# The weight split's subtractions all on VectorE, GpSimd without them: a two-block transformer on one core

## The chip, the cores and the metric

The kernel runs on 1 core of one Trainium2 chip. The metric is the device time of a launch in microseconds (us), median of the runs. A core has TensorE (PE in the rows; PEld is its weight load), VectorE (DVE), ScalarE (ACT), GpSimd (POOL), SyncE (SP, which issues the DMAs here) and 16 DMA engines.

## The reference, cut to what matters

Two blocks of two layers follow each other on 256 tokens of 1024 channels, all in float32. The second block holds the places that the prediction speaks of:

```python
for l in range(DEPTH):
    mod = cond @ ada_w[l] + ada_b[l]
    sh1, sc1, g1, sh2, sc2, g2, sh3, sc3, g3 = jnp.split(mod, N_MOD, axis=-1)
    hn = _modulate(_rms_norm(h, norm_g[l, 0]), sh1, sc1)
    h = h + 0.5 * g1[:, None, :] * _swiglu(hn, ffn1_w_in[l], ffn1_w_out[l])
    hn = _modulate(_rms_norm(h, norm_g[l, 1]), sh2, sc2)
    z = hn @ w_in[l]
    ...
    mixed = jnp.concatenate([o_a, o_b, o_c, o_d], axis=-1)
    h = h + g2[:, None, :] * (mixed @ w_out[l])
    hn = _modulate(_rms_norm(h, norm_g[l, 2]), sh3, sc3)
    h = h + 0.5 * g3[:, None, :] * _swiglu(hn, ffn2_w_in[l], ffn2_w_out[l])
```

`o_a` is a differential attention (two softmaxes, one subtracted from the other), `o_b` a causal depthwise convolution of 31 taps with a layer norm, `o_c` a spatial gating within chunks of 128 tokens, `o_d` an attention with forget gates. The first block (three attentions side by side, a gated sum and a squared-ReLU MLP) is computed ahead of it in the same way.

## The kernel before, in words

**Weights.** Activations lie feature-major, 128 channels by 256 tokens to a tile. Every weight is read from HBM once, in the order of use. `_plan` and `_subs` cut the weights into 627 parts of at most 1024 columns. A part goes through three steps. `load_to` (line 214) issues its DMA from SyncE into a tile `raw`, of which there are 5. `split_to` (line 223) makes two tiles of it, of 4 buffers each: `wh` is a rounded copy, a cast on ScalarE (line 231), and `wl` is the rest, `raw - wh` (line 233). `mm3` (line 284) then multiplies three times into the same PSUM bank: `wh` by the high part of the activation, `wh` by its low part, and `wl` by the high part. So TensorE needs `wl` of a part in the third matmul of its first group.

**Which engine subtracts.** Line 233 stands on GpSimd where `(i + 1) % prog["pool"] == 0`, else on VectorE. `prog["pool"]` is set along the program: no part on GpSimd in the first stretch, then every third, and in a feed-forward part (`ffn`, line 1108, at the last of its four output products) every part after the first feed-forward of a layer and every second after the second one. So throughout a mixer all parts are subtracted on GpSimd, until line 1378, near its end, sets every third again.

**What runs ahead.** `chunk` (line 268) hands out the parts of a product and has each part split 3 parts ahead of its use. After each part `fill` gives a step to the background pieces that are due. A framework puts the instructions of each engine into one order, by when it reckons that each can start, and it sets the semaphores. An engine works through its own order without overtaking. Where a part's subtraction stands thus moves its neighbours too.

**The mixer** (`mixer`, line 1124) runs between the two feed-forwards of a layer, twice in all. It reads two small tensors (`v2` at line 1127, `ws` at 1128), clears the convolution's input (`yv`, line 1130, held behind the last subtraction that went to VectorE), and takes from `v2` the products `lp` (line 1137). `normalised` (line 1019) writes the normalised input `xn` (line 1037). TensorE then makes the projections, and beside them run as background pieces: `qknorm` (line 1162; the tiles `qu`, `qr`, `qk`), the convolution `conv` (line 1174; 62 steps on `cv` on VectorE, then the matmuls `cc`), `diff` (line 1223; scores `ds`, probabilities `dp`, factors `drc`), `fox` (line 1266; decays `lfr`, scores `fs`) and `spatial` (line 1329). The last projection is `mv`, in 48 matmuls of 512 columns. Before the mixer `gated_update` (line 1057) adds the feed-forward's product `fd` into `x`, and TensorE sums squares into `nrm` for the norm.

**ada.** During the feed-forwards `ada_step` (line 535) takes a 512 KB tile by a DMA of SyncE and multiplies it on VectorE, 144 times in all. Line 172 is the matmul that all products go through, line 185 is `scalar_tensor_tensor`, line 188 a multiplication, line 191 an addition, line 194 a subtraction and line 600 a maximum, all on VectorE.

Of the kernel before, what the change touches and what calls it, by code (L numbers as in the profile page):

```python
# [15 lines left out]
ALU = mybir.AluOpType  # L16
# [10 lines left out]
POOL_EVERY = 3  # L27
# [51 lines left out]
def _subs():  # L79
    """The parts in which the weights are loaded and split: (chunk, first k tile, k tiles, columns, offset)."""  # L80
    subs, o = [], 0
    for j, (_, _, _, kk, _, cc) in enumerate(_plan()):
        per = max(1, SUB_COLS // cc)
        for k in range(0, kk, per):
            n = min(per, kk - k)
            subs.append((j, k, n, cc, o))
            o += P * n * cc
    return subs
# [34 lines left out]
def tile_model(ctx: ExitStack, tc: tile.TileContext, xT: bass.AP, pos: bass.AP, cvec: bass.AP, wst: bass.AP,  # L123
# [55 lines left out]
    def base_table(last):  # L179
        """Back to the table with both Exp and Ln once the given activation is issued."""  # L180
        with tc.issue_after(last.ins):
            nc.scalar.preload_act_table_set("natural_log_exp_and_others")
# [29 lines left out]
    prog = {"raw": 0, "split": 0, "chunk": 0, "fill": 0, "turn": 0, "pool": POOL_EVERY, "ada": 0}  # L212
# [10 lines left out]
    def split_to(s, ahead=5):  # L223
        while prog["split"] < min(s, len(subs)):
# [7 lines left out]
            eng = nc.gpsimd if (i + 1) % prog["pool"] == 0 else nc.vector  # L232
            ins = eng.tensor_tensor(out=wl[:, :n * cc], in0=src, in1=wh[:, :n * cc].bitcast(F32), op=ALU.subtract)  # L233
            if eng is nc.vector:
                prog["dve"] = ins.ins
# [5 lines left out]
    def fill():  # L241
        """One step of each background part that is due."""
        prog["fill"] += 1
        for g in list(bgs):
            if prog["fill"] >= due[g]:
                step(g)

    def step(g):
        """A part yields the number of fills until its next step."""
        try:  # L250
            due[g] = prog["fill"] + next(g)
        except StopIteration:
            bgs.remove(g)
# [37 lines left out]
    def gemm(chunks, ah, al, outs, klast, koff=0, after=None):  # L291
        """Feature-major product; outs[m] = (bank, half) for column tile m of each chunk."""
# [9 lines left out]
    def gemm_last(c, a, banks, klast, done):  # L302
        """The last part of a product, bank by bank, each followed by what takes it up."""
# [9 lines left out]
    def gemm_tok(chunks, ah, al, outs, klast):  # L313
        """Token-major product; outs[t] = (bank, first column)."""
# [7 lines left out]
    def gemm_shift(c, xa, banks, after):  # L322
        """The product with an unnormalised activation; the shift's products follow in two more columns."""
# [40 lines left out]
    def accumulate(n, j, t):  # L364
        """Sums of squares over the channels of a partition; the last part stays apart."""
# [15 lines left out]
    class Act:  # L381
        """A feature-major activation of n tiles as high and low float32r parts."""
# [13 lines left out]
    class Shifted:  # L396
        """An activation scaled per channel, in two parts, with two more columns for the shift."""
# [32 lines left out]
    prog["pool"] = len(subs)  # L430
# [8 lines left out]
    prog["pool"] = POOL_EVERY  # L439
# [151 lines left out]
    def pv(bank, v, pts):  # L591
        """Two heads; columns of each part: keys0 x (q0, q1), keys1 x q1."""
# [11 lines left out]
    def causal_scores(parts):  # L604
        """Masked scores of several heads: (bank, queries, keys) of each."""
# [14 lines left out]
    # =================== block 1 ===================  # L620
# [3 lines left out]
    for l in range(L):  # L624
# [361 lines left out]
        for half in range(2):  # L986
# [5 lines left out]
            for m in range(4):  # L992
# [5 lines left out]
                elif half:  # L998
                    if m == 2:
                        prog["pool"] = 3  # L1000
# [13 lines left out]
    # =================== block 2 ===================  # L1014
# [4 lines left out]
    def normalised(dst, l, i, first=False):  # L1019
        """rmsnorm(x) * g * (1 + scale) + shift in two parts, and the factor of the unnormalised product."""  # L1020
# [52 lines left out]
    def ffn(l, f, i, xa, first=False):  # L1073
# [5 lines left out]
        prog["pool"] = POOL_EVERY  # L1079
# [24 lines left out]
        for m in range(4):  # L1104
            if m == 2:
                prog["ada"] = 0
            if m == 3:
                prog["pool"] = 1 if i == 0 else 2
# [15 lines left out]
    def mixer(l, xa):  # L1124
# [253 lines left out]
        prog["pool"] = 3  # L1378
# [156 lines left out]
```

## Time and profile before

| | us |
|---|---|
| median of 3 runs | 2057.26 |
| lowest and highest of them | 2048.43, 2058.85 |
| profiled execution, span of its instructions | 2054.9 |

The profiled execution has no time of its own beside its span. The median lies 2.4 us above the span. In a row of the profile, "x" and a number is a count, a "<-" in an instruction leads from its output to its inputs, and a "<-" behind an idle time names the instruction that ended it. PEclk is the share of TensorE's full clock that was granted: 1.00 is 2.4 GHz and 0.50 is 1.2 GHz. A count of a window is of the instructions that touch it.

### The profile page before, as it was taken

How to read it: one execution, taken by the hardware profiler on the slowest of the kernel's cores; microseconds unless marked ns; L12 is line 12 of the kernel's file. 1: busy time of each engine (PE TensorE's matmuls, PEld its weight loads, DVE VectorE, ACT ScalarE, POOL GpSimd, SP SyncE). 2: the span in 40 equal slices, each digit the busy share in tenths (PEclk: the TensorE clock that was granted, in tenths of full speed). 3: DMA queues.
4: the chain of work that ended last, by engine and by line, in shares of the span. 5: the costliest groups of instructions: out<-in, count | busy, mean ns of one | idle time of the engine just before them, and what ended most of it. 6: DMA issues, size and time to landing. Idle time of an engine off the chain costs nothing. (4 is left out here: it accounts for less than half of the span.)

```text
span 2054.9 us, 38413 instructions
## 1 busy us (share of the span) xinstructions
PE 1966.4 (96%) x15570; PEld 1894.0 (92%) x15570; DVE 1480.6 (72%) x2076; ACT 1045.8 (51%) x1584; POOL 717.9 (35%) x339
## 2 busy tenths in 40 slices
PE   8999999999999999999999978998999998789999
PEld 7989999999989999999999966898999998679999
DVE  6778778696667778699877598888574446968443
ACT  5656555445556545345444446644454444455442
POOL 3232242323331343334223653422332246443222
PEclk9999999999999999999999989999999999899999
DMA  7545556885445656886667522388546554324553
GB/s 248 169 165 207 209 175 244 306 317 206 144 144 190 227 188 227 309 295 216 242 260 252 183 93 93 124 289 302 183 151 215 179 178 134 108 93 165 184 175 125
DMA packets 114946, 406.52 MB, mean 198 GB/s; under 512 B 12880, under 2 KB 14672, under 8 KB 114768
## 3 DMA queue, kind: packets, MB, share of 16 engines
q1 hardware_dynamic: 114768, 404.06, 56.6%
q8 instruction: 122, 2.00, 0.4%
q14 instruction: 56, 0.46, 0.1%
HBM read 402.96 MB, written 1.05 MB: 197 GB/s over the span
## 5 line engine op out<-in xcount | busy, mean ns | idle before, releaser
L233 POOL TENSOR_TENSOR wl<-raw,wh 128x1024 fp32r<-128x1024 f32 (+2 forms) x253 | 635.0, 2514 | 1257.7 <-ACT wh L231 1182.8
L231 ACT CAST wh<-raw 128x1024 fp32r<-128x1024 f32 (+1 forms) x627 | 641.4, 1030 | 614.7 <-PE fd L172 113.4
L233 DVE TENSOR_TENSOR wl<-raw,wh 128x1024 fp32r<-128x1024 f32 (+1 forms) x374 | 497.3, 1335 | 248.6 <-ACT wh L231 246.1
L172 PE MATMUL f<-hh,wl 128*128 128x256 f32 x1280 | 363.9, 285 | 4.9 <-POOL wl L233 4.0
L172 PE MATMUL f<-hl,wh 128*128 128x256 f32 x1280 | 364.2, 285 | 3.2 <-DVE hl L194 2.9
L172 PE MATMUL f<-hh,wh 128*128 128x256 f32 x1280 | 363.1, 284 | 4.3 <-ACT hh L203 3.1
L185 DVE SCALAR_TENSOR_TENSOR ada<-ada,cond 128x1024 f32<-128x1024 f32 x144 | 227.8, 1585 | 94.9 <-DMA ada<-ada_dram 94.6
L172 PEld LDWEIGHTS f<-hh,wl 128*128 128x128 f32 x1280 | 246.8, 193 | 6.4 <-POOL wl L233 4.6
L172 PEld LDWEIGHTS f<-hl,wh 128*128 128x128 f32 x1280 | 246.9, 193 | 4.8 <-DVE hl L194 4.8
L172 PEld LDWEIGHTS f<-hh,wh 128*128 128x128 f32 x1280 | 246.6, 193 | 5.1 <-ACT hh L203 3.7
L172 PE MATMUL fd<-hidh,wl 128*128 128x256 f32 x704 | 200.4, 285 | 4.0 <-DVE wl L233 3.5
L172 PE MATMUL fd<-hidh,wh 128*128 128x256 f32 x704 | 200.0, 284 | 0.6 <-DVE x L185 0.6
L172 PE MATMUL fd<-hidl,wh 128*128 128x256 f32 x704 | 199.9, 284 | 0.0
L172 PE MATMUL pr<-hh,wh 128*128 128x256 f32 x672 | 194.8, 290 | 0.0
L172 PE MATMUL pr<-hh,wl 128*128 128x256 f32 x672 | 190.1, 283 | 0.0
L172 PE MATMUL pr<-hl,wh 128*128 128x256 f32 x672 | 190.0, 283 | 0.0
L172 PE MATMUL dn<-hidh,wl 128*128 128x256 f32 x512 | 146.2, 285 | 3.6 <-DVE wl L233 3.6
L172 PE MATMUL u<-hh,wl 128*128 128x256 f32 x512 | 145.9, 285 | 2.6 <-DVE wl L233 2.6
L172 PE MATMUL u<-hh,wh 128*128 128x256 f32 x512 | 145.9, 285 | 0.0
L172 PE MATMUL dn<-hidh,wh 128*128 128x256 f32 x512 | 145.6, 284 | 0.0
L172 PE MATMUL dn<-hidl,wh 128*128 128x256 f32 x512 | 145.5, 284 | 0.0
L172 PE MATMUL u<-hl,wh 128*128 128x256 f32 x512 | 145.5, 284 | 0.0
(474 smaller groups left out, 4786.1 us busy)
## 6 DMA issues: line engine op xcount, KB each, us to landing
raw<-wst_dram SPq DMA_DIRECT2D x599, 512.0 KB, 4.0
ada<-ada_dram SPq DMA_DIRECT2D x144, 512.0 KB, 5.0
raw<-wst_dram SPq DMA_DIRECT2D x22, 256.0 KB, 2.8
raw<-wst_dram SPq DMA_DIRECT2D x4, 390.0 KB, 3.0
R<-ret_dram SPq DMA_DIRECT2D x2, 512.0 KB, 7.7
out_dram<-x SPq DMA_DIRECT2D x8, 128.0 KB, 3.3
C<-cst_dram SPq DMA_DIRECT2D x1, 896.0 KB, 7.7
v<-vec_dram SPq DMA_DIRECT2D x2, 448.0 KB, 5.7
```

The source lines that it names most:

```text
L172: nc.tensor.matmul(out, lhsT=lhsT, rhs=rhs, start=grp not in self.open, stop=stop, skip_group_check=True)
L185: nc.vector.scalar_tensor_tensor(out=out, in0=in0, scalar=s, in1=in1, op0=op0, op1=op1, **kw)
L231: nc.scalar.copy(wh[:, :n * cc], src)
L233: ins = eng.tensor_tensor(out=wl[:, :n * cc], in0=src, in1=wh[:, :n * cc].bitcast(F32), op=ALU.subtract)
```

## The change

`POOL_EVERY` and `prog["pool"]` go, with all places that set it. Line 233 becomes a `tensor_tensor` of VectorE for every part, and `prog["dve"]` is the last such subtraction always. Docstrings and comments go too; by that, and by the lines that went, lines stand 1 to 12 lower in number (the subtraction on line 231, `scalar_tensor_tensor` on 184, the matmul on 171).

```diff
@@ -24,7 +24,6 @@
 SUB_COLS = 1024
-POOL_EVERY = 3
 MLA_SCALE = (64 + 32) ** -0.5
...
@@ -203,13 +202,13 @@
...
-    prog = {"raw": 0, "split": 0, "chunk": 0, "fill": 0, "turn": 0, "pool": POOL_EVERY, "ada": 0}
+    prog = {"raw": 0, "split": 0, "chunk": 0, "fill": 0, "turn": 0, "ada": 0}
...
@@ -229,24 +228,22 @@
             wl = wp.tile([P, SUB_COLS], F32R, tag="wl", bufs=4, name=nm("wl"))
             src = raws.pop(i)[:, :n * cc]
             nc.scalar.copy(wh[:, :n * cc], src)
-            eng = nc.gpsimd if (i + 1) % prog["pool"] == 0 else nc.vector
-            ins = eng.tensor_tensor(out=wl[:, :n * cc], in0=src, in1=wh[:, :n * cc].bitcast(F32), op=ALU.subtract)
-            if eng is nc.vector:
-                prog["dve"] = ins.ins
+            ins = tt(out=wl[:, :n * cc], in0=src, in1=wh[:, :n * cc].bitcast(F32), op=ALU.subtract)
+            prog["dve"] = ins.ins
...
@@ -427,7 +424,6 @@
     h = Act(8, "h")
-    prog["pool"] = len(subs)
...
-    prog["pool"] = POOL_EVERY
...
@@ -996,8 +991,6 @@
                 elif half:
-                    if m == 2:
-                        prog["pool"] = 3
...
@@ -1076,7 +1069,6 @@
         gemm_shift(("F" + f, l, 0, 8, 0, 512), xa, b4, lambda: next(nrm))
-        prog["pool"] = POOL_EVERY
...
@@ -1104,8 +1096,6 @@
-            if m == 3:
-                prog["pool"] = 1 if i == 0 else 2
...
@@ -1375,7 +1365,6 @@
-        prog["pool"] = 3
```

In the whole program VectorE's order grows from 1746 to 2022 rows and GpSimd's falls from 316 to 63, with no `wl` left on it. What stays on GpSimd are sums of squares, masks, copies and maxima. ScalarE has 48 table loads where it had 42, three more in each mixer. On SyncE the loads of `raw` that waited for GpSimd to be done with a buffer wait for VectorE, and at 5 places a load of `raw` and a load of `ada` next to it change places.

**VectorE, middle of the mixer of layer 0,** at the normalisation of the second of the four query and key products (`cv` a step of the convolution, `qu` and `qr` the inverse root, `qk` its result). Before:

```order
L185 SCALAR_TENSOR_TENSOR cv_13772<-yv_13554,cw,cv_13772 128x256 x8
L185 SCALAR_TENSOR_TENSOR qu_13970<-qn_13967,eps,qr_13969 128x512
L185 SCALAR_TENSOR_TENSOR cv_13772<-yv_13554,cw,cv_13772 128x256
L185 SCALAR_TENSOR_TENSOR qu_13970<-qu_13970,qr_13969 128x512
L185 SCALAR_TENSOR_TENSOR cv_13772<-yv_13554,cw,cv_13772 128x256
L185 SCALAR_TENSOR_TENSOR qr_13969<-qu_13970,qr_13969 128x512
L185 SCALAR_TENSOR_TENSOR cv_13772<-yv_13554,cw,cv_13772 128x256
L185 SCALAR_TENSOR_TENSOR qk_13741<-qk_13851,V,qr_13969 128x512
```

Now:

```order
L184 SCALAR_TENSOR_TENSOR cv_13772<-yv_13554,cw,cv_13772 128x256 x2
L231 TENSOR_TENSOR wl_13936<-raw_13781,wh_13935 128x1024
L184 SCALAR_TENSOR_TENSOR cv_13772<-yv_13554,cw,cv_13772 128x256 x4
L184 SCALAR_TENSOR_TENSOR qu_13970<-qn_13967,eps,qr_13969 128x512
L231 TENSOR_TENSOR wl_13980<-raw_13815,wh_13979 128x1024
L184 SCALAR_TENSOR_TENSOR qu_13970<-qu_13970,qr_13969 128x512
L184 SCALAR_TENSOR_TENSOR cv_13772<-yv_13554,cw,cv_13772 128x256
L184 SCALAR_TENSOR_TENSOR qr_13969<-qu_13970,qr_13969 128x512
L184 SCALAR_TENSOR_TENSOR cv_13772<-yv_13554,cw,cv_13772 128x256
L184 SCALAR_TENSOR_TENSOR qk_13741<-qk_13851,V,qr_13969 128x512
```

Of the mixer's subtractions 16 (13 of 1024 columns, 2 of 780, 1 of 520) now stand on VectorE between the norm's inverse root and the last step on `cv`; two are seen here. By the same ordering 16 small steps of other pieces (6 on `lfr`, 1 reciprocal, 4 batch-norm statistics, 1 on `drc`, 4 on `dp`) stand ahead of the last step on `cv` where they stood behind it.

**VectorE, from the end of the first feed-forward into the mixer of layer 0** (`x` the update by the product `fd`, `xl` the low part of the scaled input, `lp` the products that read `v2`). Before:

```order
L185 SCALAR_TENSOR_TENSOR x<-fd_13196,hg_164,x 128x256 x2
L185 SCALAR_TENSOR_TENSOR xl_12813<-x,scl_162,xh_12810 128x256 x2
L1130 MEMSET yv_13554 128x576
L188 TENSOR_TENSOR lp_13562<-v_2050_13552 128x32 x2
L1138 TENSOR_REDUCE ls_13563<-lp_13562 128x1 x2
L185 SCALAR_TENSOR_TENSOR x<-fd_13375,hg_164,x 128x256 x2
L188 TENSOR_TENSOR ws_13553<-ws_13553,C 128x128 x3
L185 SCALAR_TENSOR_TENSOR xl_12813<-x,scl_162,xh_12811 128x256
```

Now:

```order
L231 TENSOR_TENSOR wl_13499<-raw_13376,wh_13498 128x1024
L231 TENSOR_TENSOR wl_13529<-raw_13406,wh_13528 128x1024
L1120 MEMSET yv_13554 128x576
L231 TENSOR_TENSOR wl_13590<-raw_13436,wh_13589 128x1024
L184 SCALAR_TENSOR_TENSOR x<-fd_13375,hg_164,x 128x256 x2
L187 TENSOR_TENSOR ws_13553<-ws_13553,C 128x128
L184 SCALAR_TENSOR_TENSOR xl_12813<-x,scl_162,xh_12811 128x256
L187 TENSOR_TENSOR ws_13553<-ws_13553,C 128x128 x3
L184 SCALAR_TENSOR_TENSOR xl_12813<-x,scl_162,xh_12811 128x256
L187 TENSOR_TENSOR lp_13562<-v_2050_13552 128x32 x2
```

The last two updates of `x` stood behind `lp`; now `lp` stands behind them.

**TensorE, end of the projections of the same mixer** (`hh_13579` holds the first four tiles of the input, `hh_13580` the last four; `cc` is the convolution's centring, `tr` a transpose). Before:

```order
L172 MATMUL mv_14402<-wh_14320,hh_13579 128x512
L172 MATMUL mv_14402<-wh_14320,hl_13581 128x512
L172 MATMUL mv_14402<-wl_14321,hh_13579 128x512
L172 MATMUL cc_14453<-cv_13772,C 128x256 x4
L588 MATMUL tr_14461<-C,dp_14092 128x128 x3
L588 MATMUL tr_14466<-C,dp_14092 128x128 x3
L172 MATMUL fs_14471<-fqk_13742 128x128
```

Now:

```order
L171 MATMUL mv_14402<-wh_14435,hh_13580 128x512
L171 MATMUL mv_14402<-wh_14435,hl_13582 128x512
L171 MATMUL mv_14402<-wl_14436,hh_13580 128x512
L171 MATMUL cc_14453<-cv_13772,C 128x256 x4
L583 MATMUL tr_14461<-C,dp_14092 128x128 x3
L583 MATMUL tr_14466<-C,dp_14092 128x128 x3
L171 MATMUL fs_14471<-fqk_13742 128x128
```

Before, `cc` stood after the first 24 of the 48 matmuls of `mv`; now it stands after all 48. The mixer of layer 1 has the same moves at all three places.

## Rows read from the trace of the kernel before

**Rows 1.** The page, part 1: busy us, share of the span, instructions of each engine.

```profile
PE 1966.4 (96%) x15570; PEld 1894.0 (92%) x15570; DVE 1480.6 (72%) x2076; ACT 1045.8 (51%) x1584; POOL 717.9 (35%) x339
```

**Rows 2.** Windows: busy (count) of PE, PEld, DVE, ACT, POOL; PEclk, DMA share, GB/s.

```profile
1600.00:1700.00 100.00, 100.00 (x836) 100.00 (x835) 46.41 (x55) 47.42 (x67) 38.36 (x20) 1.00 0.52 174
1165.00:1305.00 140.00, 114.86 (x772) 101.04 (x772) 121.94 (x237) 73.06 (x148) 68.00 (x27) 0.89 0.30 99
```

**Rows 3.** Waits of TensorE, whole span: us in total, times, longest us.

```profile
PE ds L172 <- DVE qk L185: 17.7, 2, 8.9
PE cc L172 <- DVE cv L185: 9.3, 2, 4.7
PE nrm L172 <- ACT sq L378: 8.0, 5, 2.9
PE fs L172 <- DVE lfr L1273: 6.3, 2, 3.5
...
PE f L172 <- POOL wl L233: 4.0, 2, 2.0
...
PE dn L172 <- DVE wl L233: 3.6, 3, 2.0
PE fd L172 <- DVE wl L233: 3.5, 3, 2.2
```

**Rows 4.** Groups by form, whole span: busy us, mean ns | idle before it, releasers.

```profile
L233 POOL TENSOR_TENSOR wl<-raw,wh 128x1024 fp32r<-128x1024 f32 x236 | 609.5, 2585 | 1227.2 <-ACT wh L231 1152.3 <-DVE hidl L194 29.3 <-DVE Q L188 9.8
L233 DVE TENSOR_TENSOR wl<-raw,wh 128x1024 fp32r<-128x1024 f32 x363 | 489.8, 1354 | 241.6 <-ACT wh L231 239.2 <-PE fd L172 0.3
```

**Rows 5.** Windows, first mixer, 1170.6 to 1252.1: all engines; then line L233 alone (DVE, POOL).

```profile
1170.60:1252.10 81.50, 64.91 (x436) 57.82 (x436) 80.75 (x143) 39.06 (x73) 43.20 (x16) 0.88 0.29 98
...
1170.60:1252.10 81.50, 0.00 (x0) 43.20 (x16) 0.88 0.29 98
```

**Rows 6.** Groups by form of VectorE in 1170.6 to 1252.1.

```profile
L185 DVE SCALAR_TENSOR_TENSOR cv<-yv,cw,cv 128x256 f32<-128x256 f32 x60 | 36.9, 660 | 0.0
L1037 DVE TENSOR_SCALAR xn<-xn,scl,mods 128x256 f32<-128x256 f32 x8 | 9.2, 1200 | 0.0
L185 DVE SCALAR_TENSOR_TENSOR qr<-qu,qr 128x512 f32<-128x512 f32 x4 | 6.9, 1725 | 0.0
L185 DVE SCALAR_TENSOR_TENSOR qu<-qu,qr 128x512 f32<-128x512 f32 x4 | 4.9, 1232 | 0.0
...
L1237 DVE TENSOR_SCALAR drc<-drc,lam 128x2 f32<-128x2 f32 x3 | 2.9, 963 | 0.0
```

**Rows 7.** Timeline of VectorE, single places: start us, us, instruction.

```profile
1219.21 0.68 DVE L185 SCALAR_TENSOR_TENSOR qr<-qu,qr 128x512 f32<-128x512 f32 x1
...
1220.87 2.84 DVE L185 SCALAR_TENSOR_TENSOR cv<-yv,cw,cv 128x256 f32<-128x256 f32 x7
...
1249.13 0.21 DVE L1237 TENSOR_SCALAR drc<-drc,lam 128x2 f32<-128x2 f32 x1
...
1302.63 1.22 DVE L233 TENSOR_TENSOR wl<-raw,wh 128x1024 fp32r<-128x1024 f32 x1
...
1321.94 1.38 DVE L1037 TENSOR_SCALAR xn<-xn,scl,mods 128x256 f32<-128x256 f32 x4
```

**Rows 8.** Windows, tile mv alone: busy (count) of PE, PEld, DVE, ACT.

```profile
1200.00:1305.00 105.00, 13.13 (x48) 9.58 (x48) 1.29 (x5) 1.38 (x3) 0.90 0.30 102
```

**Rows 9.** Timeline of VectorE, end of the first ffn1 [idle before, releaser].

```profile
1164.43 2.28 DVE L188 TENSOR_TENSOR lp<-v 128x32 f32<-128x32 f32 x2 [12.60 <-DMA v<-vec_dram]
...
1166.86 0.87 DVE L185 SCALAR_TENSOR_TENSOR x<-fd,hg,x 128x256 f32<-128x256 f32 x2
```

**Rows 10.** Timeline of ScalarE, one table load.

```profile
1189.37 1.28 ACT L182 ACT_TABLE_LOAD   x1
```

**Rows 11.** Windows: a stretch behind a GpSimd wait of ffn2, layer 0; columns as in rows 2.

```profile
1422.20:1425.60 3.40, 3.40 (x19) 3.40 (x18) 3.40 (x7) 1.62 (x3) 0.00 (x0) 0.50 0.53 180
```

**Rows 12.** Waits of VectorE, whole span: us in total, times, longest us.

```profile
DVE wl L233 <- ACT wh L231: 246.1, 150, 5.5
```


## The prediction

> **What bounds the kernel now.** The page's first part comes first: TensorE is busy for 1966.4 of 2054.9 us, VectorE for 72%, GpSimd for 35% [rows 1]. That looks as if little could be had from the split. The windows by stage correct it. In a feed-forward TensorE runs 836 matmuls in 100 us without a pause, at the full 2.4 GHz. In the mixer's 140 us it runs 772, is busy for 114.86, and its granted clock falls to a mean of 0.89, while VectorE is busy for 121.94 [rows 2]. TensorE's waits over the whole span say what it waits for there: `ds` for `qk`, `cc` for `cv`, `fs` for `lfr`, each twice, once in each mixer, and `nrm` for the squares, 2.9 at the longest, in the same places. Per mixer that is 8.9 + 4.7 + 3.2 + 2.9 = 19.7 us [rows 3]. Elsewhere only small waits for `wl` are left.
>
> So the question is what sets VectorE's pace in the mixer. From 1170.6 to 1252.1, which ends where `cc` gets its last `cv`, VectorE is busy for 80.75 of 81.5 us, so its work is the path there; in the same stretch GpSimd works 43.2 us on 16 subtractions [rows 5]. The groups of that stretch show four kinds of instruction well above the same instruction elsewhere: `qr` takes 1.725 us in the mean [rows 6] and 0.68 in a place where no subtraction of GpSimd runs beside it [rows 7]. **VectorE stands still while GpSimd subtracts**, and these stalls are written into its own busy time. The program's 236 full-size subtractions on GpSimd take 2.585 us each; VectorE's own take 1.354 [rows 4], and 1.22 alone [rows 7].
>
> **The change part by part.** Per mixer, with both mixers alike:
>
> (a) *Subtractions out of GpSimd, into VectorE's chain.* The stall that goes is what each group takes above its undisturbed twin: `cv` 36.9 - 60 x 0.406 = 12.5 (the twin is 2.84 / 7); `xn` 9.2 - 8 x 0.345 = 6.4 (1.38 / 4); `qr` 6.9 - 4 x 0.68 = 4.2; `qu` 4.9 - 4 x 0.68 = 2.2 (same form as `qr`); `drc` 2.9 - 3 x 0.21 = 2.3 [rows 6, 7]. Together 27.6 us. Added are 16 subtractions at 1.22 or less, 19.5 us. Net **-8.1 us** on the chain. The bounds: -27.6, if all 16 found idle time of VectorE, which 80.75 of 81.5 excludes nearly, and +19.5, if no stall went.
>
> (b) *The update of x ahead of `lp`.* Before, the last two updates of x stood behind `lp`, which waited 12.60 us for its DMA until 1164.43 and then took 2.28; the updates began only at 1166.86 [rows 9], and the norm needs their squares. In the new order `lp` stands behind them, so its DMA delays them no more. I take the whole wait of `nrm`, **-2.9 us** [rows 3]. Bounds: 0, if the subtractions now ahead of the updates fill the same time, and -2.9. What is late next is `lp` itself, whose result is needed only at `drc`, over 60 us on.
>
> (c) *Small steps moved ahead of the last `cv`.* 16 of them, by the shortest such row, 0.21 us for `drc` [rows 7]: **+3.4 us** on the way to `cc`. Bounds 0 and 16 x 0.406 = 6.5, as if each were a `cv`.
>
> (d) *Matmuls moved ahead of `cc`.* 24 of `mv` now stand before it. A row gives 13.13 us for 48, so 24 are 6.6 us [rows 8]. They fill time in which TensorE stood waiting for `cv`; the wait that they replace is 4.7 [rows 3]. Between these two I take **-5.5 us**, as they can also stand in for part of the `fs` wait.
>
> (e) *Three more table loads on ScalarE* at 1.28 us [rows 10], 3.84 together. ScalarE is busy for 39.06 of the 81.5 [rows 5], so half of them should find idle time: **+2 us**, bounds 0 and 3.84.
>
> (f) *The clock.* A mean of 0.89 over 140 us means 0.11 x 140 = 15.4 us of work lost to the stretches at 1.2 GHz [rows 2]. They stand right behind the long waits. The waits shrink but do not all go; I give back a fifth, **-3 us**. Bounds 0 and -15.4.
>
> The sum per mixer: -8.1 - 2.9 + 3.4 - 5.5 + 2 - 3 = **-14.1 us**, -28.2 for both.
>
> *Elsewhere* VectorE takes on the rest of the 253 subtractions, 236 of them of full size [rows 4], and loses the stalls. With a 2.585 us subtraction on GpSimd against one of 1.22 on VectorE, its load hardly changes, and TensorE, without a pause there, hides what does. What is left is TensorE's waits: 4.0 us for a `wl` of GpSimd goes, as that subtraction halves. Behind the second of these waits TensorE ran 3.40 us at 0.50 [rows 11], which is 1.7 of lost work. Of the 3.6 + 3.5 us for a `wl` of VectorE I take a third, 2.4, since casts and loads that come late make such waits too [rows 3]. Together **-8.1 us**. Bounds 0 and -12.8.
>
> The new wait: SyncE's loads of `raw` wait for VectorE to be done with the buffer where they waited for GpSimd, and the `ada` loads stand behind them in the same queue. As a subtraction ends earlier on VectorE than on GpSimd, I cost this at nothing; if VectorE is behind, it is the rival below.
>
> Sum: -28.2 - 8.1 = -36.3. The profiled span of 2054.9 becomes 2018.6. The median stands 2.4 above that span, so the time is **2021 us**.
>
> **The rivals.**
>
> *More than that.* The four waits of a mixer go wholly: 2 x 19.7 = 39.4; half of the clock's loss comes back, 15.4 for both mixers; with the 8.1 elsewhere this is -62.9, **1994 us**. For it: the four hang on one VectorE chain. Against it: that chain stays full, and it gets only 8.1 us shorter before (c) and (e).
>
> *The chain alone.* Only (a) comes: 2 x -8.1 = -16.2, **2041 us**. The reordering (b, d) is then eaten by (c), (e) and subtractions that stand ahead of the updates.
>
> *Nothing to be measured.* VectorE exchanges stalls for subtractions and TensorE's 96% hides the rest: **2057 us**. For it: 27.6 and 19.5 are near each other, and a subtraction of 1.22 stands in one piece before a `cv` of 0.41. Against it: 19.7 us of TensorE's waits per mixer end on this chain.
>
> *Slower, by the queue of VectorE.* On GpSimd a subtraction that waits for its cast delays no one. In VectorE's order everything behind it waits too. VectorE waits for casts already, 246.1 us in 150 waits, 1.64 each [rows 12]. With 16 such waits in a mixer's chain, 26.2 us, a mixer gains 14.1 and loses 26.2, +12.1; both +24.2, less 8.1 elsewhere: 2054.9 + 16.1 + 2.4 = **2073 us**. It decides from 14.1 / 16 = 0.88 us a subtraction on, where a mixer's gain is gone. Against it: in the new order the subtractions stand among ready `cv` steps, and a cast is three parts ahead of its use, so it should be done when its turn comes.
>
> *Slower, by a full VectorE.* The stalls may have another cause than GpSimd's subtractions, and then nothing of (a)'s 27.6 comes back: a mixer's -14.1 becomes +13.5, both +27, and with nothing elsewhere 2054.9 + 27 + 2.4 = **2084 us**. The rows on `qr` speak against it: 1.725 and 0.68 differ by the neighbour alone.
> The Trainium skill (Perfetto Trace Analysis, Optimizing Scalar/DVE Operations) says that with a saturated VectorE it may make sense to hand work to ScalarE or even GpSimd, which is this rival; the same paragraph adds that GpSimd and VectorE share a read port, so that moving work between the two might not help. The trace agrees with the second half: 1.725 beside 0.68 us for one form.
>
> That the change does not do what it says is excluded: no `wl` is left on GpSimd in the new order.
>
> **How the numbers follow.** The forecast (2003 to 2040) gets 0.60, since the terms of the chain all come from rows of one stretch; more than that 0.10; the chain alone, 2040 to 2047, 0.07; nothing to be measured 0.12; the queue 0.07; the full VectorE 0.04. The sign of the chain hangs on 27.6 against 19.5, which a third off the first would turn, hence 0.23 for the last three. The range, 1994 to 2054, holds the forecast, the chain alone, half of "more" and about half of "nothing": 0.60 + 0.07 + 0.05 + 0.06 = 0.78, some 8 in 10. A measurement of this kernel can tell 0.5%, 10.3 us, from no change. Faster by more: 0.60 + 0.10 + 0.07 = 0.77. Within it: 0.12. Slower by more: 0.07 + 0.04 = 0.11.
>
> **What would show it.** In the profile of the changed kernel VectorE's busy time should be within 30 us of 1480.6, with `qr` and `qu` at 0.68, `cv` at 0.41 and a full-size subtraction at 1.2 (a). The wait of `nrm` should be gone (b), that of `cc` be under 2 us (d), and that of `ds` be shorter than 8.9. The mixer's 140 us should be about 126, its clock above 0.89 (f). Wrong would be: `cv` still at 0.66 with GpSimd idle (full VectorE); VectorE idle in the mixer, waiting for casts, by more than 0.88 us a subtraction (queue); a mixer that is shorter while a feed-forward gets longer, by loads that wait for VectorE.

## The result, and the profile after

The changed kernel takes 1988.43 us (median of 4 runs, 1986.56 to 1991.63) against 2055.06 for the kernel before beside it; the ratio is 0.9683, interval 0.9665 to 0.97. It is 66.6 us faster, where 36 were forecast, and lies below the range.

The page's first part of the changed kernel, beside [rows 1]:

```profile
PE 1948.8 (98%) x15570; PEld 1879.0 (94%) x15570; DVE 1485.2 (75%) x2329; ACT 1056.5 (53%) x1590; POOL 85.6 (4%) x86
```

VectorE's busy time is the same within 5 us, and GpSimd's 718 are down to 86. TensorE is busy for 17.6 us less on the same work, and idle for 41.1 us where it was for 88.5. So 47 us of the gain are waits that went, and 18 us are shorter busy time on the same 15570 matmuls, while the mean granted clock of the span rose from 0.981 to 0.994.

Where that went, by windows whose bounds are the norms' matmuls: of the kernel before, the MLP of block 1's layer 0 and the first feed-forward of block 2 (both have ada steps), then the two mixers; then the same four of the kernel after. Columns as in [rows 2].

```profile
307.20:504.80 197.60, 193.88 (x1591) 192.94 (x1590) 150.52 (x166) 93.05 (x113) 62.78 (x27) 0.99 0.76 273
960.60:1164.90 204.30, 197.35 (x1598) 195.33 (x1597) 145.79 (x193) 93.33 (x139) 71.54 (x33) 0.98 0.66 236
1164.90:1316.00 151.10, 124.50 (x847) 110.22 (x845) 132.58 (x254) 81.05 (x163) 74.86 (x33) 0.90 0.31 103
1709.60:1860.80 151.20, 123.20 (x847) 108.55 (x845) 131.68 (x253) 81.01 (x163) 74.98 (x33) 0.90 0.31 104
```

```profile
305.60:496.90 191.30, 191.30 (x1591) 191.17 (x1590) 148.96 (x188) 93.08 (x113) 6.33 (x5) 1.00 0.81 279
948.30:1142.80 194.50, 193.61 (x1598) 192.38 (x1597) 147.76 (x225) 96.30 (x142) 4.31 (x5) 1.00 0.72 249
1142.80:1275.20 132.40, 119.72 (x839) 104.75 (x838) 117.12 (x275) 84.18 (x163) 4.37 (x5) 0.96 0.36 115
1662.80:1796.40 133.60, 119.91 (x840) 104.68 (x839) 117.19 (x274) 84.54 (x164) 4.37 (x5) 0.96 0.35 114
```

The two mixers gained 18.7 and 17.6 us. The two other stages gained 6.3 and 9.8 with VectorE's busy time within 2 us of what it was, and TensorE now stands still for at most 0.9 us in them. Two more stages with ada steps, the MLP of block 1's layer 1 (181.6 to 177.2) and the second feed-forward of block 2's layer 0 (201.4 to 195.8), gained in the same way.

TensorE's waits of the kernel after, whole span, beside [rows 3]:

```profile
PE mv L171 <- DVE wl L231: 6.7, 6, 2.5
PE nrm L171 <- POOL ssum L371: 3.7, 2, 1.9
PE f L171 <- DVE wl L231: 3.1, 5, 0.8
...
PE ds L171 <- ACT dp L597: 1.5, 2, 1.1
PE cc L171 <- DVE cv L184: 1.4, 2, 0.8
```

What stood for `ds`, `cc` and `fs` is nearly gone; `mv` waits 6.7 us for `wl` instead, and `nrm` 3.7 for GpSimd's sums.

VectorE's groups by form in the stretch of the mixer that answers to [rows 6], 1148 to 1225, and its window up to the start of `cc`, beside [rows 5]:

```profile
L184 DVE SCALAR_TENSOR_TENSOR cv<-yv,cw,cv 128x256 f32<-128x256 f32 x60 | 26.0, 476 | 0.0
L231 DVE TENSOR_TENSOR wl<-raw,wh 128x1024 fp32r<-128x1024 f32 x14 | 17.0, 1215 | 0.0
...
L1030 DVE TENSOR_SCALAR xn<-xn,scl,mods 128x256 f32<-128x256 f32 x8 | 2.8, 408 | 0.0
L184 DVE SCALAR_TENSOR_TENSOR qr<-qu,qr 128x512 f32<-128x512 f32 x4 | 2.7, 683 | 0.0
L184 DVE SCALAR_TENSOR_TENSOR qu<-qu,qr 128x512 f32<-128x512 f32 x4 | 2.7, 683 | 0.0
...
L231 DVE TENSOR_TENSOR wl<-raw,wh 128x780 fp32r<-128x780 f32 x2 | 1.9, 960 | 0.0
...
L1227 DVE TENSOR_SCALAR drc<-drc,lam 128x2 f32<-128x2 f32 x4 | 0.9, 218 | 0.0
...
L231 DVE TENSOR_TENSOR wl<-raw,wh 128x520 fp32r<-128x520 f32 x1 | 0.7, 685 | 0.0
```

```profile
1148.00:1224.20 76.20, 69.12 (x437) 58.77 (x436) 73.11 (x174) 49.09 (x90) 0.00 (x0) 0.93 0.34 110
```

`qr` and `qu` take 0.683 us, `xn` 0.35 (2.8 / 8), `drc` 0.218, `cv` 0.43 (26.0 / 60). The stalls left the stretch as forecast, 16 subtractions came in ahead of the last `cv` (13 of the 14 of 1024 columns, two of 780, one of 520), and VectorE is still busy for 73.11 of 76.20 us.

### The profile page after: what moved, and what is told of

It is laid out like the page before. It is cut to its first block, busy times and chain, and to the rows that moved or that the text cites. A ratio compares the mean times of both kernels' runs of the same rounds, so it can differ in the third digit from the quotient of the medians.

```text
span 1989.9 us, 38234 instructions
## 1 busy us (share of the span) xinstructions
PE 1948.8 (98%) x15570; PEld 1879.0 (94%) x15570; DVE 1485.2 (75%) x2329; ACT 1056.5 (53%) x1590; POOL 85.6 (4%) x86
## 4 chain that ended last, share of the span: by engine, by line
PE 85%; DVE 9%; ACT 2%; issue 2%; DMA 1%; SPq 0%; POOL 0%; POOLq 0%; DVEq 0%; ACTq 0%
PE f L171 22%; PE fd L171 13%; PE pr L171 12%; PE u L171 9%; PE dn L171 9%; PE br L171 3%; DVE wl L231 2%; PE wo L171 2%; DVE cv L184 2%; PE a L171 1%; PE mo L171 1%; PE sbv L171 1%; PE rv L171 1%; PE uq L171 1%; PE z L171 1%
## 5 line engine op out<-in xcount | busy, mean ns | idle before, releaser
L231 DVE TENSOR_TENSOR wl<-raw,wh 128x1024 fp32r<-128x1024 f32 (+1 forms) x627 | 756.0, 1211 | 318.2 <-ACT wh L230 316.4
L184 DVE SCALAR_TENSOR_TENSOR ada<-ada,cond 128x1024 f32<-128x1024 f32 x144 | 176.6, 1227 | 70.6 <-DMA ada<-ada_dram 70.2
L171 PEld LDWEIGHTS fd<-hidh,wh 128*128 128x128 f32 x704 | 135.2, 192 | 0.8 <-DVE x L184 0.8
```

Source lines behind the costliest of these rows:

```text
L171: nc.tensor.matmul(out, lhsT=lhsT, rhs=rhs, start=grp not in self.open, stop=stop, skip_group_check=True)
L184: nc.vector.scalar_tensor_tensor(out=out, in0=in0, scalar=s, in1=in1, op0=op0, op1=op1, **kw)
L231: ins = tt(out=wl[:, :n * cc], in0=src, in1=wh[:, :n * cc].bitcast(F32), op=ALU.subtract)
```

## The experiments

Three theories stood against each other. **Stalls:** VectorE stands still while GpSimd subtracts, and that costs everywhere. **Delay:** a part that GpSimd subtracts is ready late, with its buffers. **Order:** the moves around `lp`, `mv` and `cc` brought part of it. The table gathers what the runs gave (the kernel before beside them had medians from 2053.84 to 2058.06); its stage times lie between the first matmuls of the norms (for the end of a mixer the four that take in the last squares), "ada stages" are the four stages named above.

In the edits "..." stands for lines that are cut. Where an edit has `prog["pool"]`, it is made to the kernel before. In the runs with idle work, with the second subtraction and with the late `wl`, the cut lines give every subtraction to VectorE, as in the changed kernel, and `prog["pool"]` only marks the 253 parts that GpSimd used to subtract.

| run | time, us | VectorE busy | both mixers | ada stages |
|---|---|---|---|---|
| before | 2055.06 | 1480.6 | 302.3 | 785.0 |
| the change | 1988.43 | 1485.2 | 266.0 | 758.8 |
| mixer only | 2016.48 | 1471.8 | 266.1 | 780.0 |
| all but the mixer | 2023.20 | 1498.5 | 301.2 | 757.5 |
| idle subtraction, four pieces | 2085.15 | 1687.3 | 326.7 | 787.9 |
| idle subtraction, two pieces | 2033.28 | 1583.1 | 299.4 | 762.6 |
| idle memsets | 1994.21 | 1487.1 | 270.5 | 757.8 |
| subtracted twice on VectorE | 2071.20 | 1755.9 | 316.2 | 780.4 |
| late `wl` | 1993.08 | 1482.6 | 269.8 | 757.4 |
| idle subtraction, full width | 2148.57 | 1798.6 | 350.1 | 813.5 |
| zeros from GpSimd | 1939.71 | 1207.8 | 225.2 | 752.4 |

### The mixers alone, and all but them

```diff
-                prog["pool"] = 1 if i == 0 else 2
+                prog["pool"] = len(subs) if i == 0 else 2
```

(`len(subs)` puts no part on GpSimd.)

> Only the parts from the last product of a first feed-forward through the mixer go to VectorE; every other part stays where it was. If what the change gains adds up stage by stage, this is worth what the two mixers gained in the traces (151.1 to 132.4 and 151.2 to 133.6, together 36.3 us): about 2019 us, ratio 0.982, and the feed-forwards and the first block keep their times. If the mixers gained because the weights ran ahead from the stages before, they gain less than 25 us here.

2016.48 us, ratio 0.9824 (0.9806 to 0.9842).

The complement sets every other rule to `len(subs)` and keeps 1 for the mixers.

> The complement: VectorE subtracts everywhere, except from the last product of a first feed-forward to the end of the mixer, where GpSimd does. If it adds up, it is worth what the other stages gained in the traces, 65.0 - 36.3 = 28.7 us: about 2026 us, ratio 0.986, with mixers of about 151 us. By the prediction's term for these stages it would be worth 8.1 us, 2047 us, and the rest of the gain would hang on the mixers.

2023.20 us, ratio 0.9857 (0.9838 to 0.9875). Against 2053.84 beside them the two gain 37.4 and 30.6 us, together 68.0 where the whole change gained 66.6: the gain adds up by stage. Outside the mixers it is nearly four times the 8.1 of the prediction.

### Stalls alone: GpSimd subtracts for no one

```diff
...
+            if (i + 1) % prog["pool"] == 0:
+                jk = wp.tile([P, 256], F32, tag="jk", bufs=1, name=nm("jk"))
+                for q in range(0, n * cc, 256):
+                    w_ = wh[:, q:min(q + 256, n * cc)].bitcast(F32)
+                    nc.gpsimd.tensor_tensor(out=jk[:, :min(256, n * cc - q)], in0=w_, in1=w_, op=ALU.subtract)
```

> The changed kernel, with its order on VectorE, ScalarE and TensorE, and beside it GpSimd subtracts wh from itself, for each part that it used to split, in pieces of 256 columns into a small tile that nothing reads. No one waits for GpSimd's result, only a wh buffer is held. Stalls (VectorE stands still while GpSimd reads): VectorE gets back some 27 us of stalls per mixer on top of the 16 subtractions it now has, so the mixers are longer than before the change, over 150 us each, and the whole is above 2040 us. Duration (GpSimd's 2.4 us per subtraction made wl late): nothing waits for it now, so 1988 us within 5. Order (what moved around): also 1988.

2085.15 us, ratio 1.0159 (1.0133 to 1.0185): 97 us above the changed kernel, with its order. But four pieces took 4.1 us of GpSimd, more than a real subtraction, and ScalarE waited 28.0 us for `wh` that they held. So the dose was matched better:

```diff
...
+                w_ = wh[:, 0:256].bitcast(F32)
+                nc.gpsimd.tensor_tensor(out=jk, in0=w_, in1=w_, op=ALU.subtract)
+                nc.gpsimd.tensor_tensor(out=jk, in0=jk, in1=jk, op=ALU.subtract)
```

> As the idle subtraction before it, but the dose is matched: per part two idle pieces of 256 columns on GpSimd, some 2.1 us by that run's 1.035 us a piece (it had four, 4.1 us, beside the 2.4 to 2.6 us of a real GpSimd subtraction), and only the first reads wh, so that it holds no one up for long. The orders on VectorE, ScalarE and TensorE are those of the changed kernel. Stalls: half of the 97 us that four pieces cost, about 2036 us; the stages with ada steps and the mixers are both longer than in the changed kernel. If the held wh buffers made the cost of four pieces, under 2000 us.

2033.28 us, ratio 0.9897 (0.988 to 0.9915), 45 above the changed kernel. The mixers lose 33, the ada stages only 3.8. VectorE had lost just 98 us here, though, little more than a third of the 273 that go with GpSimd's wide reads in the run with zeros below. In the traces of all runs with idle work TensorE, VectorE and ScalarE go through their instructions in the order of the changed kernel, so none of these differences is one of order.

### Work of GpSimd that only writes

```diff
...
+                w_ = wh[:, 0:8].bitcast(F32)
+                nc.gpsimd.tensor_tensor(out=jk[:, 0:8], in0=w_, in1=w_, op=ALU.subtract)
+                for _ in range(8):
+                    nc.gpsimd.memset(jk, 0.0)
```

> The same places, but GpSimd writes only: a read of 8 columns of wh for the pace, then eight memsets of 256 columns into the tile that nothing reads. If VectorE stands still for GpSimd's reads, the time is that of the changed kernel, 1988 us within 6, with VectorE's groups at their short durations although GpSimd is busy. If any work of GpSimd stalls it, above 2020 us.

1994.21 us, ratio 0.9699 (0.9676 to 0.9721), which overlaps the changed kernel's. The page's first part and two groups by form, of GpSimd and of VectorE:

```profile
PE 1949.2 (98%) x15570; PEld 1878.6 (94%) x15570; DVE 1487.1 (75%) x2329; ACT 1058.1 (53%) x1590; POOL 916.9 (46%) x2363
```

```profile
L239 POOL MEMSET jk<- 128x256 f32 x2024 | 635.0, 314 | 115.2
```

```profile
L185 DVE SCALAR_TENSOR_TENSOR cv<-yv,cw,cv 128x256 f32<-128x256 f32 x120 | 51.7, 473 | 0.0
```

GpSimd is busy for 916.9 us, more than before the change, and VectorE's 1487.1 are those of the changed kernel; `cv` has its short duration. ScalarE waits here 123.7 us for `wh` that GpSimd's pieces hold, and nothing comes of it, so that the held buffers of the runs above cost nothing either. GpSimd's work as such stalls no one; its wide reads do.

### VectorE subtracts twice

```diff
...
+            if (i + 1) % prog["pool"] == 0:
+                ins = tt(out=wl[:, :n * cc], in0=src, in1=wh[:, :n * cc].bitcast(F32), op=ALU.subtract)
+                prog["dve"] = ins.ins
```

> The changed kernel with the subtraction done twice on VectorE for each part that GpSimd used to split, into the same tile: 253 subtractions of some 1.2 us more, about 300 us more of VectorE's time, which is what the stalls took before, and a wl that is ready 1.2 us later, but GpSimd idle. If a subtraction on GpSimd costs by the VectorE time that it takes away, this is near the kernel before: 2040 to 2065 us. If it is the lock's place (an instruction of the chain caught in the middle) that costs, it is clearly less than that: under 2020 us.

2071.20 us, ratio 1.0083 (1.0064 to 1.0102): 0.8% slower than before, and 6 us beyond the expected range. VectorE is not free to take just any load: 271 us more of work cost 83 us.

### Delay without reads, and reads without delay

```diff
...
+            own = (i + 1) % prog["pool"] == 0
+            m = n * cc - 8 if own else n * cc
+            ins = tt(out=wl[:, :m], in0=src[:, :m], in1=wh[:, :m].bitcast(F32), op=ALU.subtract)
...
+                for _ in range(3):
+                    nc.gpsimd.memset(jk, 0.0)
+                nc.gpsimd.tensor_tensor(out=wl[:, m:m + 8], in0=src[:, m:m + 8], in1=wh[:, m:m + 8].bitcast(F32),
+                                        op=ALU.subtract)
```

> GpSimd's delay without its reads. For each part that GpSimd used to split, VectorE subtracts all but the last 8 columns, and GpSimd does these 8 after a small read of wh and three memsets: some 0.79 + 3 x 0.314 + 0.79 = 2.5 us after the cast, what a real subtraction there took, with raw and wl held as long. The order on the engines is the changed kernel's but for a few small steps. If the late wl or the late raw buffer was what cost outside the mixers, the stages outside lose up to the 28.7 us that they had gained, 2005 to 2020 us. If VectorE's stalls cost there too, the time stays near the run with memsets, 1988 to 1998 us.

1993.08 us, ratio 0.9699 (0.9675 to 0.9723). The ada stages take 757.4 us, not more than with the change. The delay fell as a theory. It was somewhat smaller than planned: the last small subtraction took 0.448 us, not 0.79, so some 2.2 us in all.

```diff
...
+                jk = wp.tile([P, 512], BF16, tag="jk", bufs=1, name=nm("jk"))
+                nc.gpsimd.tensor_tensor(out=jk, in0=wh[:, 0:512].bitcast(F32), in1=C[:, 0:512], op=ALU.subtract)
+                nc.gpsimd.tensor_tensor(out=jk, in0=C[:, 0:512], in1=C[:, 0:512], op=ALU.subtract)
```

> GpSimd's reads at full dose without its delay: the changed kernel, and per such part two idle pieces of 512 columns from a constant (the first reads wh too, for the pace), some 2.4 us together, like the real subtraction; nothing waits for the result. VectorE should lose near the 305 us that it lost before, on top of all 627 subtractions, so its busy time rises from 1485 towards 1750 us. If stalls cost outside the mixers too, the stages with ada steps (from 305.6 to 496.9, 772.1 to 948.3, 948.3 to 1142.8 and 1275.2 to 1471.0 in the changed kernel) lose 15 us or more together and the whole is above 2060 us; if only the delay did, they lose under 5 and the whole is 2035 to 2050 us by the mixers alone.

2148.57 us, ratio 1.0452 (1.0422 to 1.0483). Its page's first part and GpSimd's two groups:

```profile
PE 2007.6 (93%) x15570; PEld 1917.7 (89%) x15570; DVE 1798.6 (84%) x2329; ACT 1052.9 (49%) x1590; POOL 933.1 (43%) x592
```

```profile
L236 POOL TENSOR_TENSOR jk<-wh,C 128x512 bf16<-128x512 f32 x253 | 470.2, 1858 | 1110.6 <-ACT wh L231 1088.1 <-ACT lu L1322 7.7 <-ACT sph L731 6.7
L237 POOL TENSOR_TENSOR jk<-C 128x512 bf16<-128x512 f32 x253 | 372.5, 1472 | 19.8
```

VectorE's busy time rose by 313 us for 843 us of such reads (470.2 + 372.5; 3.3 us a part, more than the 2.4 planned), the ada stages lost 54.7 and the mixers 84. The stalls cost outside the mixers too.

### The kernel before, without GpSimd's reads

```diff
...
+                nc.gpsimd.tensor_tensor(out=jk[:, 0:8], in0=src[:, 0:8], in1=w_, op=ALU.subtract)
+                nc.gpsimd.memset(jk, 0.0)
+                for q in range(0, n * cc, 256):
+                    nc.gpsimd.memset(wl[:, q:min(q + 256, n * cc)].bitcast(F32), 0.0)
```

> The kernel before, but where GpSimd subtracted it now writes zeros: a read of 8 columns for the pace and five memsets of 256 columns, some 2.4 us like the real subtraction; it leaves out the product of wl for these 253 parts. VectorE keeps its 374 subtractions and nearly its order, GpSimd its parts and its delay; only GpSimd's wide reads are gone. VectorE's busy time should fall by the stalls, from 1481 to some 1190 us. If the reads alone cost what the change gained outside the mixers, the four stages with ada steps take about 759 us together, as in the changed kernel, where they took 785 before. If the order or GpSimd's share as such cost it, they stay above 775. In the mixers, with 27 us of stalls gone and no subtraction added, under 133 us each, and the whole 1960 to 1985 us.

1939.71 us, ratio 0.9433 (0.9418 to 0.9449), below the range expected. The page's first part:

```profile
PE 1924.1 (99%) x15570; PEld 1865.5 (96%) x15570; DVE 1207.8 (62%) x2076; ACT 1048.1 (54%) x1584; POOL 513.1 (26%) x1580
```

The run leaves out the products of `wl` for these parts: TensorE does the same 15570 matmuls, some of them on zeros. It has nearly the order of the kernel before (some 140 of VectorE's 2076 instructions stand elsewhere), and GpSimd is still in the chain, with 1.75 us a part (442 us over 253) where it had 2.51. VectorE's busy time is 273 us shorter and the kernel 117; the mixers, at 112.1 and 113.1, brought most of what lies below the range. The ada stages take 752.4, less than with the change. Together with the late `wl` that settles the part outside the mixers: neither order nor GpSimd's delay cost there, the reads did.

### lp behind the updates of x

```diff
...
-            mul(lp[:, i * 32:(i + 1) * 32], lv[:, 64 * i:64 * i + 32], lv[:, 64 * i + 32:64 * i + 64])
+            with tc.issue_after(prog["upd"]):
+                mul(lp[:, i * 32:(i + 1) * 32], lv[:, 64 * i:64 * i + 32], lv[:, 64 * i + 32:64 * i + 64])
```

(`prog["upd"]` is the last update of `x`.)

> The kernel before, with lp alone put behind the last two updates of x, as in the changed kernel; engines and subtractions as before. If the wait of nrm was the update standing behind lp, its 2.9 us goes twice, with the clock that falls behind it up to 1.7 each: 2046 to 2050 us, ratio about 0.996. If the update is late for another reason, no change and the wait of nrm stays at 2.9.

2054.41 us, ratio 1.0007 (0.9992 to 1.0022): no change. A wait of TensorE in the kernel before, which stands beside [rows 3]; TensorE's waits now; and one row of VectorE's timeline, where the mixer begins:

```profile
PE qk L172 <- ACT hh L203: 4.2, 3, 1.9
```

```profile
PE ds L172 <- DVE qk L185: 15.5, 2, 8.9
PE qk L172 <- ACT hh L203: 9.2, 4, 3.1
...
PE nrm L172 <- ACT sq L378: 2.2, 3, 0.8
```

```profile
1164.29 2.97 DVE L188 TENSOR_TENSOR ws<-ws,C 128x128 f32<-128x128 f32 x3 [3.25 <-DMA ws<-wsT_dram]
```

The wait of `nrm` fell from 8.0 us to 2.2, and that of `qk` for the normalised input grew from 4.2 us to 9.2: VectorE now waits for the DMA of `ws` (3.25 us) and takes 2.97 for it, stalls included. The wait moved.

### Two versions that go further

```diff
-            nc.gpsimd.tensor_tensor(out=acc, in0=t[:, 0:256], in1=t[:, 256:512], op=ALU.add)
+            tt(out=acc, in0=t[:, 0:256], in1=t[:, 256:512], op=ALU.add)
...
-            nc.gpsimd.tensor_tensor(out=acc, in0=acc, in1=t[:, e * 256:(e + 1) * 256], op=ALU.add)
+            tt(out=acc, in0=acc, in1=t[:, e * 256:(e + 1) * 256], op=ALU.add)
```

> The changed kernel with GpSimd's sums of squares on VectorE as well. In the changed kernel nrm waits 1.86 us for such a sum of GpSimd at the end of each mixer. If that wait is the path, it goes: 3.7 us, with what the clock gives back up to 1.7 each: 1981 to 1985 us. Against it stand 56 additions of some 0.41 us on VectorE: if they come in the way at the norms, 1988 us or more.

1984.31 us, ratio 0.966 (0.9643 to 0.9677). No `nrm` wait for a sum is left, though the mixers did not get shorter (268.1 us for 266.0); the ada stages did (754.8 for 758.8). The interval overlaps the changed kernel's at its edge, so this step by itself is not settled.

```diff
-                nc.vector.tensor_scalar(out=t_[:, e * 256:(e + 1) * 256], in0=t_[:, e * 256:(e + 1) * 256],
-                                        scalar1=acol[:, k:k + 1],
-                                        scalar2=mods[l][:, 24 * i + k:24 * i + k + 1], op0=ALU.mult, op1=ALU.add)
+                act(t_[:, e * 256:(e + 1) * 256], t_[:, e * 256:(e + 1) * 256], AF.Identity, scale=acol[:, k:k + 1],
+                    bias=mods[l][:, 24 * i + k:24 * i + k + 1])
```

> The version with the sums of squares on VectorE, and xn's scaling (line 1030, 8 instructions of 0.35 us in each of six norms) on ScalarE. In the mixer VectorE is still the path, 73.1 of 76.2 us: 2.8 us less on it per mixer, 5.6 together, if ScalarE's turn of table loads and casts does not make it later: 1979 to 1984 us. If ScalarE is late there, 1984 us or more.

1979.34 us, ratio 0.9634 (0.961 to 0.9657), which lies wholly below the changed kernel's interval. In its first mixer VectorE is still busy for 115.41 of 130.40 us.

## Why the prediction was wrong

**The step that failed** is "Elsewhere": -8.1 us, bounds 0 and -12.8. It measured -28.7 in the two traces (65.0 less 36.3 in the mixers), and -30.6 by the run that changed only these stages. Of the 28.7 the four ada stages brought 26.2. The prediction said that VectorE's "load hardly changes, and TensorE, without a pause there, hides what does". On the load it was right in the ada stages, as the sums over their windows show, before the change, with zeros and after:

```profile
sum 785.00, PE 763.90 PEld 758.28 DVE 593.34 ACT 369.30 POOL 262.72; mean PE 190.97 PEld 189.57 DVE 148.33 ACT 92.33 POOL 65.68
```

```profile
sum 752.40, PE 751.87 PEld 750.06 DVE 484.91 ACT 372.30 POOL 180.79; mean PE 187.97 PEld 187.51 DVE 121.23 ACT 93.07 POOL 45.20
```

```profile
sum 758.80, PE 754.20 PEld 750.92 DVE 585.35 ACT 371.66 POOL 25.85; mean PE 188.55 PEld 187.73 DVE 146.34 ACT 92.91 POOL 6.46
```

VectorE's 593.3 us became 585.4, yet the time fell by 26.2. Two things were wrong in the step.

First, TensorE was not without a pause there. The window of [rows 2] that shows none lies in a feed-forward without ada steps. In the four stages with them TensorE stood still for 785.0 - 763.9 = 21.1 us before and for 4.6 after, and its busy time fell by 9.7 more, as the mean granted clock rose from 0.98 and 0.99 to 1.00. The step priced 6.4 us of waits and 1.7 of clock.

Second, it counted a microsecond in which VectorE stands still as equal to one in which it works. The run with zeros parts the two: taking the stalls out brought 32.6 us in these stages, and putting nearly as much work in cost 6.4. The table has the prices, as kernel time over VectorE's busy time, both as differences in us:

| | whole kernel | both mixers | ada stages |
|---|---|---|---|
| stalls taken out: before to zeros | 117 / 273 = 0.43 | 77.1 / 83.6 = 0.92 | 32.6 / 108.4 = 0.30 |
| work put in: zeros to the change | 48.7 / 277 = 0.18 | 40.8 / 53.6 = 0.76 | 6.4 / 100.4 = 0.06 |
| stalls put in: the change to two pieces | 45 / 98 = 0.46 | 33.4 / 30.4 = 1.10 | 3.8 / 40.3 = 0.09 |
| to four pieces | 97 / 202 = 0.48 | 60.7 / 64.6 = 0.94 | 29.1 / 88.3 = 0.33 |
| to full width | 160 / 313 = 0.51 | 84.1 / 90.8 = 0.93 | 54.7 / 130.4 = 0.42 |
| work put in: the change to twice | 83 / 271 = 0.31 | 50.2 / 58.3 = 0.86 | 21.6 / 98.3 = 0.22 |

In the mixers, where VectorE is the path, a microsecond of either costs nearly one. In the ada stages the price of stalls rises with the dose (0.09, 0.33, 0.42), and from either starting point stalls cost more than a like amount of work: 0.30 against 0.06 around the zeros (with what order and delay did in it), 0.33 against 0.22 from the change. The first of these is the difference that "Elsewhere" left out.

With the run of zeros as the point between, the change is 117 us for the stalls that it takes out, less 49 for the work (and the order) that it puts in; 41 of the 49 fall in the mixers.

How a stall turns into a wait of TensorE can be read at one place before the change; why it does so more often than work outside the mixers is argued from there and not shown. VectorE's timeline, GpSimd's and TensorE's, near 439 us in the MLP of block 1's layer 0:

```profile
433.83 2.27 DVE L185 SCALAR_TENSOR_TENSOR ada<-ada,cond 128x1024 f32<-128x1024 f32 x1 [1.07 <-DMA ada<-ada_dram]
...
436.03 0.68 DVE L194 TENSOR_TENSOR hidl<-rq,hidh 128x512 fp32r<-128x512 f32 x1
436.63 1.21 DVE L185 SCALAR_TENSOR_TENSOR ada<-ada,cond 128x1024 f32<-128x1024 f32 x1
...
437.78 1.21 DVE L233 TENSOR_TENSOR wl<-raw,wh 128x1024 fp32r<-128x1024 f32 x1
```

```profile
432.34 2.68 POOL L233 TENSOR_TENSOR wl<-raw,wh 128x1024 fp32r<-128x1024 f32 x1 [5.90 <-ACT wh L231]
```

```profile
439.04 0.52 PE L172 MATMUL dn<-hidh,wl 128*128 128x256 f32 x1 [2.01 <-DVE wl L233]
```

An `ada` step that came with its DMA at 433.83 was caught by GpSimd's subtraction, which ended at 435.02, and took 2.27 us instead of 1.21. Two more steps of VectorE stood before `wl`, which TensorE then awaited for 2.01 us. The window behind that wait, columns as in [rows 2]:

```profile
439.10:442.50 3.40, 3.40 (x16) 3.40 (x17) 3.29 (x5) 0.78 (x2) 0.00 (x0) 0.51 1.01 319
```

TensorE ran there at half its clock. Where the framework orders the instructions, a subtraction on VectorE has its place, and a stall has none.

**The mixers**, forecast -14.1 each, measured -18.7 and -17.6, and -18.6 for both alike when only they were changed (37.4 / 2). (a) The mechanism and its size were right: `cv`, `xn`, `qr`, `qu` and `drc` gave back 10.9 + 6.4 + 4.2 + 2.2 + 2.0 = 25.7 of the forecast 27.6, and 18.4 came in for the 16 subtractions ahead of the last `cv` (15.8 for 13 of 1024 columns, 1.9 for two of 780, 0.7 for one of 520), 19.5 forecast. (b) was wrong as a gain of its own: `lp` moved alone left the time unchanged. (c), (d), (e) were not tried alone. The stretch they act on took 5.3 us less (76.2 for 81.5) and held more of TensorE's work (69.12 us for 64.91, [rows 5]), with the wait of `cc` at 1.4 for two mixers. The new wait of `mv` for `wl`, 6.7 us for both, was in no term. (f) was small but near by busy time: TensorE's per mixer fell by 4.8 and 3.3 us, in part by 8 and 7 matmuls fewer in the window; the forecast gave 3. By the prediction's own product it was too small: (1 - 0.90) x 151.1 = 15.1 us became (1 - 0.96) x 132.4 = 5.3, two thirds and not a fifth. That the mixers' total came as near as it did is thus in part luck: (b) gave nothing, `mv` got a wait that was not foreseen, and the clock gave back more.

**The rivals.** "More than that", 1994 us, had the size and half of the reason: the long waits went, and the clock came back with them; but it too left the stages outside at 8.1. That its time came so near is luck: it had 54.8 us for the mixers, which brought 36.3. "The chain alone" and "nothing to be measured" fell with 1988. The queue of VectorE did not decide: VectorE waits more for casts, 316.4 us in 288 waits, 1.10 each, but of the mixer's stretch it idles for 3.1 us in all. The full VectorE fell with `qr` at 0.683.

The Trainium skill (Perfetto Trace Analysis, Optimizing Scalar/DVE Operations) has both halves of this: handing work from a saturated VectorE to another engine may make sense, but GpSimd shares a read port with it. Here the second half decided. What the first half could be worth at most shows in the run with zeros, which leaves that work out: another 49 us.

## What to carry to other kernels

Where GpSimd and VectorE both work on SBUF, compare each VectorE instruction with its twin in a place where GpSimd is idle before counting what GpSimd takes off VectorE's hands: here each of the 253 subtractions on GpSimd cost VectorE about as much time in stalls (273 us in all) as doing it (277). Price stalls by what they did to the bottleneck engine, and stage by stage, not by VectorE's busy sum: equal sums went with times 66 us apart, and the equality itself hid a fall of 30.0 us in the mixers and 8.0 in the ada stages against a rise of 42.5 in the others. Before calling a group of stages free of waits, look at each of them in a window of its own. And test a gain that is read off one wait by moving that one instruction alone: one such wait went away here and came back as another.

## What the runs showed of the hardware that was not expected

It is GpSimd's reads that stall VectorE, and not by GpSimd's busy time alone: 843 us of reads of 512 columns added 313 us to VectorE's busy time, 1017 us of reads of 256 columns (four pieces) added 202, and 635 us of memsets with 200 us of reads of 8 columns added 2. The stall spares some instructions. In the mixer before the change `qu<-qn,eps,qr`, which takes one operand from PSUM, took 741 ns and after it 744, where `qu<-qu,qr` of the same size, with both in SBUF, fell from 1232 to 683:

```profile
L185 DVE SCALAR_TENSOR_TENSOR qu<-qn,eps,qr 128x512 f32<-128x512 f32 x4 | 3.0, 741 | 0.6 <-ACT qr L562 0.6
```

```profile
L184 DVE SCALAR_TENSOR_TENSOR qu<-qn,eps,qr 128x512 f32<-128x512 f32 x4 | 3.0, 744 | 0.0
```

Few of these met a subtraction, though: 2 of the 8 in both mixers, at 747 ns. The update of `x` is the better row. It reads `fd` from PSUM, and before the change 16 of its 32 instructions ran wholly inside a subtraction of GpSimd; their mean is 479 ns, that of the 10 which met no work of GpSimd 476, and the longest of all (minimum, median, maximum in the row) took 486:

```profile
L185 DVE SCALAR_TENSOR_TENSOR x<-fd,hg,x x32: 468/476/486, 1116.4 to 2051.5; 128x256 f32<-128x256 f32 x32
```

The Trainium skill (SBUF — State Buffer, Who interferes with whom) says that a VectorE instruction with two SBUF inputs contends with a GpSimd instruction that reads SBUF and not with one that only writes it, and that one with at most one SBUF input does not contend outside certain modes, which `tensor_scalar` can enter. The traces agree with the first by `qu<-qu,qr` and the run with memsets, and with the second by the update of `x`. The `tensor_scalar` of `xn` and `drc` were slowed too (1200 to 408 ns, 963 to 218); whether by such a mode no run here shows.

GpSimd is held in turn. In the run with memsets the 7 reads of 8 columns beside which VectorE did nothing took 0.20 us each, the other 246 took 0.81 in the mean. One of each kind; the longer began just behind a subtraction of VectorE and ended with it:

```profile
42.53 1.17 POOL L237 TENSOR_TENSOR jk<-wh 128x8 f32<-128x8 f32 x1 [6.46 <-ACT wh L231]
...
453.10 0.20 POOL L237 TENSOR_TENSOR jk<-wh 128x8 f32<-128x8 f32 x1 [1.97 <-ACT wh L231]
```

```profile
42.42 1.23 DVE L232 TENSOR_TENSOR wl<-raw,wh 128x1024 fp32r<-128x1024 f32 x1 [0.31 <-ACT wh L231]
```

So the mean of a small piece of GpSimd, such as the 1.035 us of 256 columns in the run with four pieces, is no price of the piece alone: time in which VectorE held it can be in it.
